# Decays as pinned steps of the SSD order, and a third buffer for split weights, in a hybrid Conformer, Mamba-2 and PEER step

## The chip, the cores and the metric

The kernel runs on one core of a Trainium2 chip. Its time is device time in microseconds, the median of several runs of the whole program: 1510.69 us over three runs, from 1509.24 to 1513.67. Profiled executions have a time and a span of their own, given below.

## What is computed

One step of a hybrid decoder layer on 336 token columns: 8 running sequences of 8 new tokens each (64 columns), 16 meta tokens and one prompt of 256 tokens. The layer normalises the input, projects it once, runs two branches, gates and adds them, and then runs a PEER expert mixer. Cut to what matters here, in the order of the reference:

```python
proj = rmsnorm(x, norm1_w) @ w_in + b_in          # 80 blocks of 128 columns, and dt
glu_in, z, xbc, dt_raw, gate_raw = split(proj)
u = ga * sigmoid(gb)                              # Conformer branch: GLU, 31-tap depthwise
c = silu(layernorm(causal_depthwise(concat(conf_buf, u), conf_dw_w, conf_dw_b)))
xbc_c = silu(causal_depthwise(concat(mconv_buf, xbc)))   # Mamba-2 branch: 4 taps, then SSD
acs = cumsum(dt * A)
decay = exp(where(causal, acs[:, None] - acs[None], -inf))
y_diag = einsum('btsgr,bsgrp->btgrp', cb[..., None] * decay, dt * x)
y_off  = einsum('btgn,bgrpn->btgrp', Cc, hc) * exp(acs)
h_new  = exp(last) * hc + einsum('bsgn,bsgrp->bgrpn', Bc, w_end * dt * x)
y_b = gated_group_rmsnorm(y + D * x, z, m_norm_w) @ w_m_out
x = x + (g_a * y_a + g_b * y_b) @ w_o
x = x + peer(rmsnorm(x, norm2_w))
```

There are 8 SSD groups of 4 heads; a head is 64 wide and the state 128.

## The kernel before

Activations lie with features on the partitions and the 336 token columns along the free axis. Every projection is one 128-wide block of weights (512 KB) against the normalised input. To keep fp32 accuracy both sides are split in a high and a low part (tiles `wh` and `wl`, `ah` and `al`): `weight` (L237) loads the block to `wraw` (4 buffers), ScalarE casts it to `wh`, and GpSimd, or for a share of the blocks VectorE, subtracts to make `wl`; both have 2 buffers. `proj` (L230) then issues 24 matmuls into one of three `pj` PSUM buffers: 16 that read `wh`, and 8 that read `wl`.

The middle of the kernel is a loop over the 8 SSD groups. In it three threads of work are woven by hand. A generator `ssd(g)` yields between its steps. The next group's conv branch (`conf(g+1)`: a value and a gated projection, then a 31-tap convolution on VectorE, L393, of which all but the first group's is given a low priority) and its four `xbc` blocks (projection, 4-tap convolution L408, Silu) and two `z` blocks are called between the steps. So one projection stands between two steps. The old group's last two steps (its second state update, its part of the group norm) run at the start of the next group. In the eighth group, where there is no next one, gate projections and the layer norm of the conv branch take that place (`norm_mean`, `norm_var`, `norm_scale`).

A scheduler places the instructions on the engines. Three rules bind it. Inside the loop `mm` and `tr` (L149, L154) keep PE's matmuls and transposes in the order in which the program calls them (`pin`). `act` (L194) chains those ScalarE activations that need a function table in program order. All else (VectorE, GpSimd, plain ScalarE copies) is placed by the scheduler.

The decays: `decays(g)` (L492) builds, for each of the 4 heads, a PSUM tile `pdec` by two matmuls (L498, L499; a broadcast of the cumulated dt, and the causal mask), which three Exps turn into `dec`; then two more tiles (L506) for the growth factors `e2`. `pdec` shares two PSUM buffers (tag `y`) with the outputs `py` and `po` of a group, so a third decay matmul waits until the first head's Exps have read theirs. These matmuls are called by `nc.tensor.matmul`, not by `mm`, so they are not pinned; `decays(g+1)` is called after the first xbc step of group g+1, a whole group ahead, and `dec` and `e2` have two buffers.

The steps of `ssd`: `turn(i)` transposes x and B of token tile i (`ptr`) and makes `xt` (x times dt, on ScalarE, L532) and `wx` (on GpSimd); `inner(i)` multiplies `dec` by C B^T (`pcb`, L545); `state(i)` makes the prompt's running states `hs` (`pst`, L557); `running` applies the cached states `st` to C (`pq`) and decays them on GpSimd (L569); `out(b)` makes the outputs (`py`, `po`, L585, L587); `update(q)` adds to the cached states (L599). All of these small PSUM tiles but `pdec`, `py` and `po` share two `misc` buffers. At the end `gnorm_stats` (L644) makes the group norm's factors from the sums `pgn` of all groups, and `gnorm` broadcasts them (`pgb`) and applies them.

## Time and profile before

| | us |
|---|---|
| median of 3 runs | 1510.69 |
| the profiled execution's own time | 1508.3 |
| its span | 1506.5 |
| the seven loop groups with a next group | 81 to 463 |
| the eighth group, with the first gates | 463 to 505 |
| gates, output projections (PE full from 556) | 505 to 700 |

The span is the time from the first to the last instruction; the execution's own time is 1.8 us longer. PE is TensorE's matmuls, PEld its weight loads, which run beside matmuls, DVE VectorE, ACT ScalarE, POOL GpSimd, SP the engine that issues most DMAs. A row of a timeline gives the start in us from the span's start, the length in us, the engine, the line, the operation, the tiles written and read with their shape, and, in brackets, how long the engine had stood idle before and what released it. A matmul's row lasts longer than the distance to the next, since matmuls are pipelined; the distance is what counts. In a table of waits each row is the waiting engine and line, what it waited for, and the total in us, the number of times and the longest. In a table by stage the granted clock is TensorE's, as a share of full speed.

### The profile page before, as it was taken

The numbers are of one execution on the slowest core, as the hardware profiler recorded it, in microseconds if no ns is written. First come the engines' busy times: TensorE is split into PE (matmuls) and PEld (weight loads), VectorE is DVE, ScalarE is ACT, GpSimd is POOL, SyncE is SP. The second block draws the span as 40 slices with busy tenths as digits, with TensorE's granted clock in tenths as the row PEclk, the third lists the DMA queues.
The fourth block names the chain that finished last, engine by engine and source line by source line (L and its number), as shares of the span: only waits on it lengthen the run. The fifth ranks groups of instructions, "written<-read, shape, count | busy, mean of one in ns | idle before, by whom it ended". The sixth has DMA issues, their size and how long they took to land.

```text
span 1506.5 us, 24647 instructions
## 1 busy us (share of the span) xinstructions
PE 1356.1 (90%) x9308; PEld 1272.0 (84%) x9308; DVE 1008.8 (67%) x2350; ACT 540.2 (36%) x1441; POOL 575.2 (38%) x467
## 2 busy tenths in 40 slices
PE   5878877977979799999999988999988999987997
PEld 3767766866867699998989987999988999987997
DVE  6765675675582751256999997677788868776423
ACT  4666566576564744343422222112111101111001
POOL 2236545645656366575322133213223112242100
PEclk9879889989989899999999999999999999999999
DMA  5414234234333234444499989999999999999983
GB/s 192 153 61 158 83 120 165 74 133 144 106 127 113 74 131 148 142 143 158 141 394 414 414 331 416 415 403 364 417 380 417 409 368 375 383 417 416 413 333 104
DMA packets 86807, 382.05 MB, mean 254 GB/s; under 512 B 10112, under 2 KB 15360, under 8 KB 66080
## 3 DMA queue, kind: packets, MB, share of 16 engines
q1 hardware_dynamic: 64144, 226.87, 41.2%
q0 software_dynamic: 20736, 151.00, 24.6%
q10 hardware_dynamic: 1808, 2.60, 0.5%
q8 instruction: 73, 1.20, 0.3%
q14 instruction: 46, 0.38, 0.1%
HBM read 367.41 MB, written 13.03 MB: 253 GB/s over the span
## 4 chain that ended last, share of the span: by engine, by line
PE 49%; DVE 12%; DMA 7%; ACT 1%; issue 1%; POOL 0%; DVEq 0%; POOLq 0%; ACTq 0%
PE va L1277 18%; PE pj L150 14%; PE pj L1186 10%; PE pg L1215 4%; DMA eraw<-in_vE_dram 3%; DMA eraw<-in_uT_dram 3%; DVE ygat L1120 2%; DVE wuv L1112 2%; DMA nd<-x1d 1%; DVE si L922 1%; DVE cand L965 1%; PE psc L1022 1%; DVE si L919 0%; DVE cand L959 0%; DVE cand L962 0%
## 5 line engine op out<-in xcount | busy, mean ns | idle before, releaser
L1000 POOL DMA_INDIRECT wuv<-in_peer_uv_dram,gid x144 | 180.1, 1251 | 513.0 <-DVE ygat L1120 221.8
L215 POOL TENSOR_TENSOR wl<-wraw,wh 128x1024 fp32r<-128x1024 f32 x115 | 275.3, 2394 | 262.4 <-PE pj L150 125.5
L1186 PE MATMUL pj<-nd,eraw 128*128 128x176 f32 x2048 | 321.5, 316 | 12.0 <-DMA eraw<-in_uT_dram 9.1
L1277 PE MATMUL va<-S,eraw 128*128 128x176 f32 x2048 | 315.2, 314 | 12.7 <-DMA eraw<-in_vE_dram 12.7
L1186 PEld LDWEIGHTS pj<-nd,eraw 128*128 128x128 f32 x2048 | 308.0, 191 | 16.2 <-ACT S L1188 7.6
L1277 PEld LDWEIGHTS va<-S,eraw 128*128 128x128 f32 x2048 | 306.1, 190 | 17.6 <-DMA eraw<-in_vE_dram 15.9
L150 PE MATMUL pj<-ah,wh 128*128 128x336 f32 (+1 forms) x768 | 260.0, 346 | 2.1 <-ACT xnf L195 2.1
L150 PE MATMUL pj<-al,wh 128*128 128x336 f32 (+1 forms) x768 | 250.6, 333 | 0.0
L214 ACT CAST wh<-wraw 128x1024 fp32r<-128x1024 f32 x128 | 134.5, 1050 | 200.5 <-PE pj L150 120.9
L1120 DVE SCALAR_TENSOR_TENSOR ygat<-wuv,scg,ygat 128x1024 f32<-128x1024 f32 x128 | 164.0, 1281 | 50.8 <-ACT scg L1115 50.6
L1112 DVE SCALAR_TENSOR_TENSOR wuv<-wuv,x2m 128x1024 f32<-128x1024 f32 x128 | 156.0, 1219 | 40.2 <-DMA wuv<-in_peer_uv_dram,gid 40.2
L1114 ACT ACTIVATE scg<-scg 128x1 f32<-128x1 f32 x144 | 29.1, 202 | 411.5 <-DVE wuv L1112 411.4
L150 PEld LDWEIGHTS pj<-ah,wh 128*128 128x128 f32 x768 | 156.8, 204 | 15.1 <-issue 5.9
L150 PEld LDWEIGHTS pj<-al,wh 128*128 128x128 f32 x768 | 156.6, 204 | 1.0 <-DVE al L215 0.5
L393 DVE SCALAR_TENSOR_TENSOR pcv<-ccat,vec,pcv 128x272 f32<-128x272 f32 x464 | 146.6, 392 | 9.8 <-ACT pcv L391 9.8
L150 PE MATMUL pj<-ah,wl 128*128 128x336 f32 (+1 forms) x768 | 138.4, 319 | 0.0
L150 PEld LDWEIGHTS pj<-ah,wl 128*128 128x128 f32 x768 | 122.7, 189 | 0.8 <-issue 0.7
L1188 ACT ACTIVATE S<-pj 128x176 f32<-128x176 f32 x128 | 37.5, 311 | 148.0 <-PE pj L1186 148.0
L1215 PE MATMUL pg<-oh 128*128 128x64 bf16 x1056 | 75.7, 241 | 0.0
L1215 PEld LDWEIGHTS <-oh 128*128 128x128 bf16 x1056 | 71.2, 117 | 2.3
L1222 DVE TENSOR_TENSOR S<-S,pg 128x192 f32<-128x192 f32 (+1 forms) x66 | 31.6, 507 | 56.7 <-PE pg L1215 56.6
L498 PE MATMUL pdec<-acs,id 96*128 96x336 bf16 x32 | 11.9, 375 | 58.6 <-ACT dec L195 58.5
(345 smaller groups left out, 1750.4 us busy)
## 6 DMA issues: line engine op xcount, KB each, us to landing
eraw<-in_uT_dram SPq DMA_DIRECT2D x128, 512.0 KB, 13.2
eraw<-in_vE_dram SPq DMA_DIRECT2D x128, 512.0 KB, 9.3
wraw<-in_w_in_dram SPq DMA_DIRECT2D x80, 512.0 KB, 3.6
st<-in_state_dram SPq DMA_DIRECT2D x8, 1024.0 KB, 5.2
out_ssm_s_dram<-st SPq DMA_DIRECT2D x8, 1024.0 KB, 6.5
wraw<-in_w_mo_dram SPq DMA_DIRECT2D x16, 512.0 KB, 3.4
wraw<-in_w_q_dram SPq DMA_DIRECT2D x16, 512.0 KB, 3.4
wraw<-in_w_co_dram SPq DMA_DIRECT2D x8, 512.0 KB, 3.5
```

Of the source, the lines that this page charges most:

```text
L150: i_ = nc.tensor.matmul(*a_, **kw)
L214: (nc.vector.tensor_copy if on_dve else nc.scalar.copy)(h, src)
L215: (nc.gpsimd if on_pool else nc.vector).tensor_tensor(l, src, h.bitcast(F32), op=OP.subtract)
L393: t = nc.vector.scalar_tensor_tensor(o, i_, wv, a_, op0=OP.mult, op1=OP.add)
L1000: i_ = nc.gpsimd.indirect_dma_start(out=u, out_offset=None, in_=ia["peer_uv"], in_offset=bass.IndirectOffsetOnAxis(ap=gid[:, c:c + 1], axi ...
L1112: nc.vector.scalar_tensor_tensor(u[:, :D], u[:, :D], 1.0, x2m if c < NPICK else x2e, op0=OP.mult, op1=OP.mult, accum_out=w)
L1120: nc.vector.scalar_tensor_tensor(a_, u[:, D:], scg[:, c:c + 1], a_, op0=OP.mult, op1=OP.add)
L1186: i_ = nc.tensor.matmul(p[:, :ND], raw[:, k, :], nd[:, k, :], start=(k == 0), stop=(k == KD - 1))
L1188: nc.scalar.activation(Sv(b), p[:, :ND], AF.Gelu)
L1215: i_ = nc.tensor.matmul(pg[:, q, :], B[:, q // 4, :, q % 4], A[:, c_, q // 4, :, q % 4], start=(c_ == 0), stop=(c_ == 2))
L1222: nc.vector.tensor_tensor(sv_, sv_, pg.rearrange("p t i -> p i t")[:, i0:i1], op=OP.mult)
L1277: i_ = nc.tensor.matmul(va[k // 2][:, k % 2], raw[:, k, :], Sv(b), start=False, stop=(b == 127), skip_group_check=True)
```

## The change

The changed kernel computes the same. Six things differ.

1. `decays(g)` is gone. Inside `ssd(g)` stand `decay(r)` for one head and `growth(b)` for two, with `mm`, so their matmuls are pinned. The first two heads are the generator's first step, before the conv-value projection of the next group; the other two come behind `turn(0)`, after it; the two growth tiles behind `turn(2)`, after the gated projection. `dec` and `e2` have one buffer.
2. The other steps are dealt out anew: `turn(1)` and `turn(2)` together, `running` with `inner(0)`, then one `inner` and one `state` at a time. The old group's last update and its norm sum fall one projection later than before.
3. In `turn`, x times dt is one VectorE product over 4 heads where it was four ScalarE activations. In `state`, four VectorE operations per tile become one GpSimd product and one VectorE add.
4. `weight` puts the split parts of each third block in a tile pair of their own (`wh3`, `wl3`) in the pool `sp`, where the second buffers of `dec` and `e2` were.
5. In the eighth group four gates stand between the first steps, `norm_var` is cut in two, and `norm_scale` and the seventh gate come before the last two updates, not after the loop.
6. `gnorm_stats` is called after the loop by itself, no longer inside `norm_scale`.

In the program as built the line numbers of the changed kernel differ by a few; pinned decay matmuls carry L150, the line of `mm`.

On PE, inside a group of the loop. Before, at the third head of the next group (`pcb` is the group's last inner product, `pj` the projection of the first xbc block ahead of it):

```order
L150 MATMUL pj<-ah,wl 128x336 x8
L150 MATMUL pcb<-bc 128x128 x2
L498 LDWEIGHTS id_256
L498 MATMUL pdec<-acs_247,id_256 128x336
L499 LDWEIGHTS identb
L499 MATMUL pdec<-mneg,identb 128x336
```

In the changed kernel, at the third head of the group itself (`pst` is the old group's second state update, `pj` the conv-value projection, `ptr` the transposes of the first token tile):

```order
L150 MATMUL pj<-ah,wl 128x336 x8
L150 MATMUL pst_1239<-wx_712,Bm 128x256
L150 MATMUL pst_1240<-wx_712,Bm 128x256
L150 MATMUL pst_1239<-wx_712,Bm 128x256
L150 MATMUL pst_1240<-wx_712,Bm 128x256
L155 MATMUL ptr<-cst,xg 80x128 x2
L155 MATMUL ptr<-cst,bc 80x128
L150 LDWEIGHTS id_256
L150 MATMUL pdec<-acs_247,id_256 128x336
L150 LDWEIGHTS identb
L150 MATMUL pdec<-mneg,identb 128x336
```

The third head has moved from behind the first xbc projection of the group before to behind the first projection of its own group.

On ScalarE, what stands ahead of the first head's Exps. Before (`xg` is the Silu of the first xbc block; `pj<-mcat` starts its convolution, which VectorE finishes):

```order
L406 ACTIVATE pj<-mcat,vec 128x360
L195 ACT_TABLE_LOAD
L195 ACTIVATE xg<-pj 128x272
L195 ACTIVATE xg<-pj 128x64
L195 ACT_TABLE_LOAD
L195 ACTIVATE dec<-pdec,acs_199 128x80
```

In the changed kernel (`sz` is the Silu of the second z block, `sq` a square for the old group's norm):

```order
L639 ACTIVATE sq<-xg 128x336
L195 ACTIVATE sz<-pj,vec 128x336
L195 ACT_TABLE_LOAD
L195 ACTIVATE dec<-pdec,acs_199 128x80
L195 ACTIVATE dec<-pdec,acs_224 128x128
L195 ACTIVATE dec<-pdec,acs_240 128x128
```

The Exps have moved from behind a Silu that needs VectorE to behind one that reads a projection.

On VectorE, at the turn from one group to the next. Before (`st` are the four adds of the state updates, `ccat` the start of the conv branch):

```order
L599 TENSOR_TENSOR st<-st,pst_1794 128x512
L599 TENSOR_TENSOR st<-st,pst_1795 128x512
L599 TENSOR_TENSOR st<-st,pst_1833 128x512
L599 TENSOR_TENSOR st<-st,pst_1834 128x512
L641 TENSOR_TENSOR pgn<-pgn 8x336
L477 SCALAR_TENSOR_TENSOR ccat<-pj,vec,xnf 128x272
```

In the changed kernel (`cbuf` are the last taps of the long convolution, `xt` the new products):

```order
L395 SCALAR_TENSOR_TENSOR cbuf<-ccat,vec,pcv 128x272
L395 SCALAR_TENSOR_TENSOR cbuf<-ccat,vec,pcv 128x64
L597 TENSOR_TENSOR st<-st,pst_1239 128x512
L597 TENSOR_TENSOR st<-st,pst_1240 128x512
L532 TENSOR_TENSOR xt_1252<-ptr,dtok_193 80x256
L644 COPY pgn<-pgn 8x336
L479 SCALAR_TENSOR_TENSOR ccat<-pj,vec,xnf 128x272
L480 SCALAR_TENSOR_TENSOR ccat<-pj,vec,xnf 128x8x8
L532 TENSOR_TENSOR xt_1389<-ptr,dtok_218 128x256
L532 TENSOR_TENSOR xt_1398<-ptr,dtok_234 128x256
```

The long convolution's taps, which ended in the middle of a group before, now reach to the second state update, and the xt products stand beside the conv branch's start.

The diff:

```diff
--- before.py
+++ after.py
@@ -237,15 +237,16 @@
         def weight(src, i):
             raw = wp.tile([128, KD, 128], F32, name="wraw", bufs=rb[0])
             nc.sync.dma_start(raw, src[i].rearrange("p (k m) -> p k m", m=128))
-            h = wp.tile([128, KD, 128], F32R, name="wh", bufs=2)
-            l = wp.tile([128, KD, 128], F32R, name="wl", bufs=2)
+            third = extra and nw[0] % 3 == 2
+            h = extra[0].tile([128, KD, 128], F32R, name="wh3") if third else wp.tile([128, KD, 128], F32R, name="wh", bufs=2)
+            l = extra[0].tile([128, KD, 128], F32R, name="wl3") if third else wp.tile([128, KD, 128], F32R, name="wl", bufs=2)
             nw[0] += 1
             f_ = lm[0]
             on_dve = int((nw[0] + 1) * f_) > int(nw[0] * f_)
             split(h, l, raw, on_pool=not on_dve, on_dve=lm[0] == 1)
             return h, l
 
-        lm, nw = [LM[3]], [NW0]
+        lm, nw, extra = [LM[3]], [NW0], []
 
         def rows(h, l):
             return lambda k: (h[:, k, :], l[:, k, :])
@@ -364,6 +365,7 @@
...
+        extra.append(sp)
...
@@ -489,34 +491,33 @@
...
-        def decays(g):
-            dec = sp.tile([128, 4, T], F32, name="dec", bufs=2)
-            e2 = sp.tile([128, 2, T], F32, name="e2", bufs=2)
-            for r in range(4):
-                h = 4 * g + r
-                pb = ps.tile([128, T], F32, name="pdec", tag="y", bufs=2)
-                nc.tensor.matmul(pb, id3[:, h:h + 1].to_broadcast([3 * H, 128]), acs3, start=True, stop=False)
-                nc.tensor.matmul(pb, identb, mneg, start=False, stop=True)
-                for i, (t0, L) in enumerate(TILES):
-                    act(dec[:, r, t0:t0 + L], pb[:, t0:t0 + L], AF.Exp, bias=acs[i][:, h:h + 1])
-            for b in range(2):
-                pb = ps.tile([128, T], F32, name="pdec", tag="y", bufs=2)
-                for r in range(2):
-                    h = 4 * g + 2 * b + r
-                    nc.tensor.matmul(pb[r * 64:(r + 1) * 64], id3[:, h:h + 1].to_broadcast([3 * H, 64]), acs3,
-                                     start=True, stop=True)
-                act(e2[:, b], pb, AF.Exp)
-            return dec, e2
-
         def r4(ap):
             return ap.rearrange("p (r c) -> p r c", r=4)
 
-        def ssd(g, xg, bc, sz, dec, e2):
+        def ssd(g, xg, bc, sz):
             BT, CT = bc[:, 0, :], bc[:, 1, :]
             st = sp.tile([128, NQ, 256], F32, name="st", bufs=2)
             nc.sync.dma_start(st, ia["state"][g])
             cz = cq[g % 2]
             xt, wx, hs = [], [], []
+            dec = sp.tile([128, 4, T], F32, name="dec")
+            e2 = sp.tile([128, 2, T], F32, name="e2")
+
+            def decay(r):
+                h = 4 * g + r
+                pb = ps.tile([128, T], F32, name="pdec", tag="y", bufs=2)
+                mm(pb, id3[:, h:h + 1].to_broadcast([3 * H, 128]), acs3, start=True, stop=False)
+                mm(pb, identb, mneg, start=False, stop=True)
+                for i, (t0, L) in enumerate(TILES):
+                    act(dec[:, r, t0:t0 + L], pb[:, t0:t0 + L], AF.Exp, bias=acs[i][:, h:h + 1])
+
+            def growth(b):
+                pb = ps.tile([128, T], F32, name="pdec", tag="y", bufs=2)
+                for r in range(2):
+                    h = 4 * g + 2 * b + r
+                    mm(pb[r * 64:(r + 1) * 64], id3[:, h:h + 1].to_broadcast([3 * H, 64]), acs3,
+                       start=True, stop=True)
+                act(e2[:, b], pb, AF.Exp)
...
@@ -528,9 +529,8 @@
...
-                for r in range(4):
-                    nc.scalar.activation(x_[:L, r * P:(r + 1) * P], p[:L, r * P:(r + 1) * P], AF.Copy,
-                                         scale=dtok[i][:L, 4 * g + r:4 * g + r + 1])
+                nc.vector.tensor_tensor(r4(x_[:L, :256]), r4(p[:L, :256]),
+                                        dtok[i][:L, 4 * g:4 * g + 4, None].to_broadcast([L, 4, P]), op=OP.mult)
...
@@ -552,10 +552,8 @@
                 if i == 0:
                     nc.vector.tensor_copy(h_, p)
                 else:
-                    for r in range(4):
-                        c_ = slice(r * P, (r + 1) * P)
-                        nc.vector.scalar_tensor_tensor(h_[:, c_], hs[-1][:, c_], el[:, 8 + i, 4 * g + r:4 * g + r + 1],
-                                                       p[:, c_], op0=OP.mult, op1=OP.add)
+                    nc.gpsimd.tensor_tensor(r4(h_), r4(hs[-1]), decay_b(8 + i), op=OP.mult)
+                    nc.vector.tensor_tensor(h_, h_, p, op=OP.add)
                 hs.append(h_)
 
             def running():
@@ -598,28 +596,35 @@
                     sv = st[:, 4 * s_ + q:4 * s_ + q + 2].rearrange("p q c -> p (q c)")
                     nc.vector.tensor_tensor(sv, sv, pair_[s_], op=OP.add)
 
+            decay(0)
+            decay(1)
+            yield
             turn(0)
+            decay(2)
+            decay(3)
+            yield
             turn(1)
+            turn(2)
+            growth(0)
+            growth(1)
             for s_ in range(2):
                 nc.scalar.copy(cz[:, 4 * s_:4 * s_ + 4, 8 * s_:8 * s_ + 8],
                                CT[:, 32 * s_:32 * s_ + 32].rearrange("p (q t) -> p q t", q=4))
             yield
-            turn(2)
+            running()
             inner(0)
             yield
             inner(1)
+            state(0)
+            yield
             inner(2)
-            yield
-            state(0)
-            running()
-            yield
             state(1)
-            state(2)
-            nc.sync.dma_start(oa["ssm_p"][g], hs[2])
             Bm = sp.tile([S0, 4, N], F32, name="Bm")
             for r in range(4):
                 nc.scalar.activation(Bm[:, r], xt[0][:S0, 256:], AF.Copy, scale=C("segs", S0)[:, r:r + 1])
             yield
+            state(2)
+            nc.sync.dma_start(oa["ssm_p"][g], hs[2])
             out(0)
             yield
             out(1)
@@ -698,15 +703,15 @@
                 nc.scalar.activation(sq, cb[:, k, :], AF.Square)
                 squares.append(sq)
 
-        def norm_var():
-            pv.append(pj())
-            for k in range(KD):
+        def norm_var(ks):
+            if not pv:
+                pv.append(pj())
+            for k in ks:
                 mm(pv[0], ones, squares[k], start=(k == 0), stop=(k == KD - 1))
 
         def norm_scale():
             rs = tp.tile([128, T], F32, name="rs", bufs=2)
             rstd_of(rs, pv[0], D, tp)
-            r24.append(gnorm_stats())
             for k in range(KD):
                 nc.vector.tensor_tensor(cb[:, k, :], cb[:, k, :], rs, op=OP.mult)
                 act(cb[:, k, :], cb[:, k, :], AF.Silu, scale=V("ln_g", k), bias=V("ln_b", k))
@@ -723,59 +728,47 @@
         (tiles, steps), (sz, zsteps) = xbc(0), zproj(0)
         for f in steps + zsteps:
             f()
-        de = decays(0)
         lm[0] = LM[0]
         pin[0] = True
         old = iter(())
         for g in range(G):
-            new = ssd(g, *tiles, sz, *de)
+            new = ssd(g, *tiles, sz)
             if g + 1 < G:
-                ca, cg = conf(g + 1)
-                ca()
+                tiles, steps = xbc(g + 1)
+                tasks = conf(g + 1) + steps
+            else:
+                lm[0] = LM[1]
+                tasks = [lambda: gate(len(gates))] * 4
+            run(old, 1)
+            run(new, 1)
+            for f in tasks:
+                f()
                 run(old, 1)
                 run(new, 1)
-                cg()
-                run(old, 1)
-                run(new, 1)
-                tiles, steps = xbc(g + 1)
-                steps[0]()
-                run(new, 1)
-                de = decays(g + 1)
-                steps[1]()
-                run(new, 1)
-                steps[2]()
-                run(new, 1)
-                steps[3]()
-                run(new, 1)
+            if g + 1 < G:
                 sz, zsteps = zproj(g + 1)
                 zsteps[0]()
                 run(new, 1)
                 zsteps[1]()
-                run(new, 1)
                 old = new
             else:
-                lm[0] = LM[1]
-                gate(0)
-                run(old, 2)
-                run(new, 2)
-                gate(1)
-                run(new, 2)
-                gate(2)
-                run(new, 1)
-                gate(3)
-                run(new, 1)
                 norm_mean()
                 gate(4)
                 run(new, 1)
+                norm_var(range(4))
+                run(new, 1)
                 gate(5)
                 run(new, 1)
-                norm_var()
-                run(new, 2)
+                norm_var(range(4, KD))
+                norm_scale()
+                gate(6)
+                run(new, 3)
         nc.scalar.dma_start(oa["mconv"], mnew)
         ls.close()
+        extra.clear()
 
         m2 = mix.enter_context(tc.tile_pool(name="m2", bufs=1))
-        norm_scale()
+        r24.append(gnorm_stats())
         while len(gates) < NB:
             gate(len(gates))
         for g in range(G):
```

## The prediction

> **What bounds the kernel now.** I read the page first, then the table of waits, then busy times by stage, then the rows of one group. The profiled execution took 1508.3 us, its span 1506.5 us; the sum is made against 1508.3 and the median of the three runs, 1510.69, lies 2.4 us above it.
>
> ```profile
> PE 1356.1 (90%) x9308; PEld 1272.0 (84%) x9308; DVE 1008.8 (67%) x2350; ACT 540.2 (36%) x1441; POOL 575.2 (38%) x467
> ```
>
> PE is the engine to watch. Its waits, over the whole span, are led by one entry (line waited at, releaser: total us, times, longest); the third row is from the same table for all engines between 80 and 480 us:
>
> ```profile
> PE pdec L498 <- ACT dec L195: 58.5, 8, 8.5
> PE pgb L150 <- DVE acs L225: 8.2, 1, 8.2
> ...
> ACT xg L195 <- DVE pj L408: 19.5, 7, 3.2
> ```
>
> Eight times PE stands before a decay matmul for ScalarE's Exp. Busy time by stage (length, then PE, PEld, DVE, ACT, POOL, granted clock) for three of the seven loop groups and a stretch well behind them:
>
> ```profile
> 81.00:135.70 54.70, 45.66 (x300) 40.06 (x299) 34.28 (x95) 33.62 (x90) 30.51 (x30) 0.88 0.26 85
> 190.30:245.00 54.70, 46.09 (x296) 39.46 (x297) 34.28 (x96) 33.95 (x90) 30.91 (x31) 0.91 0.37 123
> 408.70:463.00 54.30, 45.36 (x292) 39.03 (x291) 33.89 (x97) 35.19 (x89) 29.58 (x27) 0.91 0.38 130
> ...
> 556.00:700.00 144.00, 143.67 (x942) 142.86 (x941) 56.63 (x70) 62.05 (x88) 92.05 (x47) 1.00 0.48 157
> ```
>
> A loop group takes (463.0 − 81.0) / 7 = 54.6 us, and no engine is busy for more than 46 of them. Behind 556 us PE is full at clock 1.00, so what the loop saves moves everything later forward by as much. Why PE stands there is read on ScalarE (start, us, engine, line, operation, then idle before and its releaser):
>
> ```profile
> 96.51 0.51 ACT L195 ACTIVATE xg<-pj 128x272 f32<-128x272 f32 x2 [3.20 <-DVE pj L408]
> 97.02 1.28 ACT L195 ACT_TABLE_LOAD   x1
> 98.32 1.57 ACT L195 ACTIVATE dec<-pdec,acs 128x80 f32<-128x80 f32 x6
> ```
>
> The Exps of the next group's first two heads stand behind the Silu of that group's first xbc tile, which waits for VectorE's short convolution, itself between taps of the long one. Two PSUM buffers hold two heads, so PE stops at the third. What a stop costs, in one group, beside one projection at full clock (the first three rows):
>
> ```profile
> 53.95 0.32 PE L150 MATMUL pj<-ah,wh 128*128 128x336 f32 x1
> 56.43 1.40 PE L150 MATMUL pj<-ah,wl 128*128 128x336 f32 x8
> 57.67 0.32 PE L150 MATMUL pj<-ah,wh 128*128 128x336 f32 x1
> ...
> 188.37 1.13 PE L150 MATMUL pst<-wx,Bm 32*128 32x256 f32 x8
> 189.43 0.32 PE L498 MATMUL pdec<-acs,id 96*128 96x336 bf16 x1
> 189.58 0.31 PE L499 MATMUL pdec<-mneg,identb 128*128 128x336 bf16 x1
> ...
> 208.83 0.44 PE L498 MATMUL pdec<-acs,id 96*128 96x336 bf16 x1 [7.88 <-ACT dec L195]
> 211.63 0.65 PE L150 MATMUL pj<-ah,wh 128*128 128x336 f32 x1
> 216.00 1.40 PE L150 MATMUL pj<-ah,wl 128*128 128x336 f32 x8
> ```
>
> A projection is 24 matmuls in 57.67 − 53.95 = 3.72 us; its first 16 take 2.48. After the 7.88 us stop the same 16 take 216.00 − 211.63 = 4.37, a loss of 1.9: PE runs slow for some 6 us. The eight decay matmuls take 2.80 where 8 x 0.15 (the spacing at 189.43) and a hop of 0.1 would be 1.3, a loss of 1.5. So a stop costs 7.88 + 1.9 + 1.5 = 11.3 us, and a group without one 54.6 − 11.3 = 43.3 us.
>
> The Trainium skill (TensorE: Matmul & The Clock Gate, on HAM oscillation) says that PE's clock halves after an idle window of some 3.4 us and comes back after a busy one. The trace agrees on the halving, not on the length of the slow stretch, 6 us here.
>
> **The change part by part.** *Decays as steps.* The same matmuls are issued, pinned, as pairs of heads with one projection between: heads 0 and 1 before the conv-value projection, 2 and 3 after it, the growth rows after the gated one. Now the Exps of heads 0 and 1 follow the Silu of the second z tile, with no VectorE work ahead of them. The same run of ScalarE work exists before the first group:
>
> ```profile
> 69.94 0.56 ACT L195 ACTIVATE sz<-pj,vec 128x336 f32<-128x336 f32 x1
> 70.51 1.28 ACT L195 ACT_TABLE_LOAD   x1
> 71.81 3.23 ACT L195 ACTIVATE dec<-pdec,acs 128x80 f32<-128x80 f32 x12
> ```
>
> Silu, load and half of the twelve Exps are 0.56 + 1.28 + 1.6 = 3.4 us, 5.0 with a weight cast (1.05) and a square (0.48) ahead. PE's cover until the third head: the update before (188.37 to 189.43, 1.06), heads 0 and 1 (0.6), a projection (3.72), the second update (1.06) and one set of transposes (0.6), 7.0 us. That leaves 2.0 us, so the stop goes. Heads 2 and 3 have the gated projection as cover for 1.6 us of Exps; the growth Exps are not needed before the outputs, four projections later. Table loads stay four a group: Exp, Sigmoid, Exp, Silu, where it was Sigmoid, Silu, Exp, Silu. One buffer for dec and e2 instead of two costs nothing: the next group's first Exp comes after the last output's matmuls and one projection (3.72).
>
> The Trainium skill (ScalarE: Activation LUTs, What ACT_TABLE_LOAD costs) gives 1.28 us for a load and 1.38 more for a drain. The trace has the load at 1.28 and the next activation 0.02 later (70.51, 71.81). By the skill's figure the margin of 2.0 would be an estimated 0.6, and the sum the same.
>
> *Who takes over work.* Groups of rows for 190.3 to 245.0 us (count, busy, mean ns, idle before):
>
> ```profile
> L393 DVE SCALAR_TENSOR_TENSOR pcv<-ccat,vec,pcv 128x272 f32<-128x272 f32 (+1 forms) x58 | 18.3, 393 | 1.1 <-ACT pcv L391 1.1
> L599 DVE TENSOR_TENSOR st<-st,pst 128x512 f32<-128x512 f32 x5 | 3.3, 683 | 8.0 <-PE pst L150 8.0
> L557 DVE SCALAR_TENSOR_TENSOR hs<-hs,el,pst 128x64 f32<-128x64 f32 x8 | 1.6, 278 | 0.4 <-PE pst L150 0.4
> L641 DVE TENSOR_TENSOR pgn<-pgn 8x336 f32<-8x336 f32 x1 | 0.5, 493 | 5.0 <-PE pgn L150 5.0
> L553 DVE COPY hs<-pst 128x256 f32<-128x256 f32 x1 | 0.4, 425 | 1.2 <-PE pst L150 1.2
> L569 POOL TENSOR_TENSOR st<-st,el 128x256 f32<-128x256 f32 x8 | 4.6, 619 | 0.0
> L532 ACT ACTIVATE xt<-ptr,dtok 128x64 f32<-128x64 f32 (+1 forms) x12 | 2.8, 322 | 0.0
> ```
>
> No row shows VectorE's new 256-wide product out of PSUM; the copy L553 has that width and source. Bounds are 0.28 (one L557) and 0.68 (512 wide, L599); I take 0.42. VectorE: + 3 x 0.42 for xt, − 1.6 for the eight state steps, + 2 x 0.42 for the two adds: 34.3 becomes 34.8 us. ScalarE loses 2.8: 34.0 becomes 31.2. GpSimd gains 2 x 0.62: 30.9 becomes 32.1. Against 43.3 that is 80%, 72% and 74%.
>
> *The third set of split weights* removes no PE wait, since none of PE's waits names wh or wl; it keeps any from coming. On GpSimd a state product now stands ahead of a weight split and waits for VectorE's add; with a third set that split is a whole projection early (3.72), more than the 0.62 of the product and an add of 0.42.
>
> *VectorE's order* is the part that is not free. Between the second state update and the conv branch's ccat it holds only an xt product and the pgn add, 1.0 to 2.2 us of work with the update's own adds, while PE needs two transposes, two heads, a projection and ScalarE's Sigmoid, some 6 us: 4 us idle each group. The other 32.6 us must fit into 43.3 − 6.0 = 37.3, a margin of 4.7 for all other hand-overs. VectorE is idle for 20.4 us of a group today; half of that would make 34.8 + 10.2 = 45.0. I take 44.7, 1.4 above PE's floor: the bounds are 43.3 and the 50.1 of three quarters, and it lies nearer the floor because the taps now stand between the hand-overs to the group's end. Loop: 7 x (54.6 − 44.7) = 69.3 us.
>
> *Start and end.*
>
> ```profile
> 72.70 0.44 PE L498 MATMUL pdec<-acs,id 96*128 96x336 bf16 x1 [3.12 <-ACT dec L195]
> 75.50 0.65 PE L150 MATMUL pj<-ah,wh 128*128 128x336 f32 x1
> 79.69 1.40 PE L150 MATMUL pj<-ah,wl 128*128 128x336 f32 x8
> ...
> 463.56 0.73 PE L150 MATMUL pgn<-sq,cstm 128*8 128x336 f32 x2 [0.86 <-DVE st L599]
> 465.91 0.44 PE L155 MATMUL ptr<-cst,xg 128*128 128x128 f32 x2 [0.49 <-ACT xt L532]
> 468.03 0.40 PE L150 MATMUL pcb<-bc 128*80 128x80 f32 x2 [1.57 <-ACT xt L532]
> 468.59 0.48 PE L150 MATMUL pj<-al,wh 128*128 128x336 f32 x1
> ```
>
> The eighth stop, before the first group, costs 3.12, then 2.80 − 1.3 and (79.69 − 75.50) − 2.48: 6.3 us; I take 5, since what starts the loop stays. In the last group the transposes wait 2.9 us for ScalarE and VectorE, and the slow projection behind adds about 1.4; spread steps remove most, 3. Against that the wait before pgb, 8.2: a gate projection stood behind the last group's end as its cover (3.72) and now stands before it, and the statistics' Ln and Exp come behind the norm's eight Silus and two table loads (2 x 1.28 at most). I take 2 us lost there, between 4 lost and 1 won. End: 1 gained.
>
> Sum: 69.3 + 5 + 1 = 75.3; 1508.3 − 75.3 = 1433.0, and 2.4 for the median: **1435.4 us**.
>
> **The rivals.** *VectorE binds.* For it: 80% busy, in order, with PE's transposes waiting for its state adds. Against: taps fill its gaps. With three quarters of today's idle time its group is 50.1 us; gains 7 x 4.5 + 6 = 37.5, so 1508.3 − 37.5 + 2.4 = 1473.2. It decides from 4.7 us of hand-overs on. By the skill's clock rule, single waits under 3.4 us leave the clock alone; the rows from 463.56 to 468.59 show three of 0.5 to 1.6 us and then half speed (0.28 us from 468.59 to the next), so I keep slow stretches in this rival.
>
> *Two stops for one, slower.* Place: the third head's matmul and the first growth one, which both wait for a PSUM buffer that an Exp must free. If ScalarE comes to the Silu more than 2.0 us late, PE stops, and if it stops at both, each group has two stops at today's price: 7 x 11.3 = 79 us more, 1508.3 + 79 + 2.4 = 1590. For it: ScalarE is in order and its weight casts wait for PE. Against: a third set frees a cast's buffer a projection earlier.
>
> *No change.* The order moves but the stop returns elsewhere at its old size, or the later stage takes the time back: 1510.7. Against it: PE at 143.67 of 144.00 us.
>
> **How the numbers follow.** Forecast 0.78, VectorE binds 0.14, no change 0.03, two stops 0.05. Best case: 7 x 11.3 + 6.3 + 4 = 89.4, so 1421; with the start's unknown order 1419. The range goes from there into the first rival, to 1474. Beyond 0.3% (4.5 us, about what a measurement of this kernel can tell): faster 0.92, same 0.03, slower 0.05.
>
> **What would show it.** Right: PE's wait at pdec under 6 us in all; group starts 44 to 46 us apart; the granted clock above 0.96 through the loop; four table loads a group; VectorE busy some 35 us a group; pgb still waiting 8 to 12 us. Wrong: groups over 48 us, PE's waits led by a transpose or state matmul behind VectorE, or clock rows still near 0.91.

## The result and the profile after

The changed kernel takes 1439.25 us (median of four runs, 1437.99 to 1442.71); the kernel before, on the same chip, 1510.24. The ratio is 0.953, with a 95% interval from 0.9506 to 0.9553. The forecast was 1435.4. Two executions among those of the versions below, one of 4575.13 us (third set late) and one of 3342.22 (no third set), were far slower than all others of their kernels, and the ratios leave them out.

The profiled execution of the changed kernel took 1442.71 us, the slowest of its four, with a span of 1440.9 and a mean granted clock of 0.973 (0.957 before). By stage, cut where PE issues the first transposes of the first and of the eighth group and the first and last output projection (the first is the one that reads `yh`, the last the one that reads `mh`):

| stage | before, us | after, us | difference |
|---|---|---|---|
| start to the first group | 80.9 | 83.4 | +2.5 |
| seven loop groups | 383.3 | 303.15 | −80.1 |
| eighth group to the first output projection | 81.5 | 88.9 | +7.4 |
| output projections | 128.4 | 128.4 | 0.0 |
| the rest, with the same code | 832.4 | 837.0 | +4.6 |

Without the last row the stages sum to −70.2, and the medians differ by 71.0. The 4.6 us of the rest are put down to these two executions: the one of the changed kernel was 3.5 us above its median, the one of the kernel before 1.9 below.

In the table of PE's waits of the changed kernel (line waited at, releaser: total, times, longest) the entry at `pdec` that led it is gone; the first of these rows was 8.2 before, the other three are new:

```profile
PE pgb L150 <- DVE acs L225: 12.0, 1, 12.0
PE ptr L155 <- DVE st L597: 5.7, 7, 1.0
PE pst L150 <- DVE st L597: 5.0, 1, 5.0
PE pj L150 <- ACT wh L214: 4.7, 1, 4.7
```

Busy time by stage after (length, then PE, PEld, DVE, ACT, POOL, granted clock): the loop, one group of it, the eighth group, and the stretch of the statistics and the last gates.

```profile
83.40:386.50 303.10, 296.83 (x2064) 261.79 (x2062) 236.05 (x646) 222.26 (x544) 217.97 (x217) 1.00 0.46 150
169.10:212.70 43.60, 42.52 (x295) 37.36 (x295) 34.50 (x94) 31.69 (x78) 30.55 (x32) 1.00 0.47 154
386.50:434.00 47.50, 41.99 (x264) 34.52 (x265) 22.69 (x40) 26.16 (x50) 24.83 (x24) 0.95 0.29 92
434.00:475.40 41.40, 27.39 (x154) 25.44 (x154) 26.71 (x47) 25.61 (x48) 17.30 (x12) 0.77 0.23 77
```

The loop, at clock 0.90 before, runs at 1.00 now, and PE is busy for 42.5 of a group's 43.6 us. ScalarE's rows of one group show why no head waits; the first two heads' matmuls were issued from 162.79 on, the last of them at 163.23:

```profile
160.59 1.05 ACT L214 CAST wh<-wraw 128x1024 fp32r<-128x1024 f32 x1 [2.42 <-PE pj L150]
161.93 0.52 ACT L195 ACTIVATE sz<-pj,vec 128x336 f32<-128x336 f32 x1
162.46 1.28 ACT L195 ACT_TABLE_LOAD   x1
163.75 1.57 ACT L195 ACTIVATE dec<-pdec,acs 128x80 f32<-128x80 f32 x6
```

The Silu is over before the first of these matmuls; the table load ends 0.2 us after the last one (163.23 + 0.31). Both heads' buffers are free at 165.32, and PE comes to the third head 4.1 us later, 0.8 of them a wait in the transposes. The third head needs the first head's buffer alone, which is free some 0.8 us earlier (half of 1.57, an estimate):

```profile
161.72 1.13 PE L150 MATMUL pst<-wx,Bm 32*128 32x256 f32 x8
...
167.17 1.13 PE L150 MATMUL pst<-wx,Bm 32*128 32x256 f32 x8
169.08 0.42 PE L155 MATMUL ptr<-cst,xg 128*80 128x128 f32 x2 [0.78 <-DVE st L597]
169.33 0.27 PE L155 MATMUL ptr<-cst,bc 128*80 128x128 f32 x1
169.44 0.31 PE L150 MATMUL pdec<-acs,id 96*128 96x336 bf16 x1
```

### The profile page after: what moved, and what is told of

Same layout as the page of the kernel before. It is cut to its first block, busy times and chain, and to the rows that moved or that the text cites. A ratio compares the mean times of both kernels' runs of the same rounds, so it can differ in the third digit from the quotient of the medians.

```text
span 1440.9 us, 24529 instructions
## 1 busy us (share of the span) xinstructions
PE 1333.8 (93%) x9308; PEld 1260.0 (87%) x9308; DVE 1004.4 (70%) x2326; ACT 525.9 (36%) x1347; POOL 587.3 (41%) x483
## 4 chain that ended last, share of the span: by engine, by line
PE 74%; DVE 14%; DMA 8%; ACT 2%; issue 1%; POOL 0%; DVEq 0%; SPq 0%; ACTq 0%
PE pj L150 31%; PE va L1270 19%; PE pj L1179 11%; PE pg L1208 4%; DMA eraw<-in_vE_dram 3%; DMA eraw<-in_uT_dram 3%; PE pst L150 2%; DVE ygat L1113 2%; DVE wuv L1105 2%; PE pdec L150 1%; PE po L150 1%; DMA nd<-x1d 1%; PE py L150 1%; PE ptr L155 1%; DVE si L915 1%
## 5 line engine op out<-in xcount | busy, mean ns | idle before, releaser
L993 POOL DMA_INDIRECT wuv<-in_peer_uv_dram,gid x144 | 184.2, 1279 | 513.1 <-DVE ygat L1113 217.5
L1179 PEld LDWEIGHTS pj<-nd,eraw 128*128 128x128 f32 x2048 | 309.7, 192 | 16.7 <-ACT S L1181 11.8
L150 PE MATMUL pj<-ah,wh 128*128 128x336 f32 (+1 forms) x768 | 249.7, 334 | 6.7 <-ACT wh L214 4.7
L150 PE MATMUL pj<-al,wh 128*128 128x336 f32 (+1 forms) x768 | 241.0, 322 | 0.0
L395 DVE SCALAR_TENSOR_TENSOR pcv<-ccat,vec,pcv 128x272 f32<-128x272 f32 x464 | 151.6, 388 | 17.7 <-ACT pcv L393 17.7
L150 PEld LDWEIGHTS pj<-ah,wh 128*128 128x128 f32 x768 | 148.0, 193 | 16.7 <-ACT wh L214 4.8
L150 PEld LDWEIGHTS pj<-al,wh 128*128 128x128 f32 x768 | 148.3, 193 | 1.1 <-DVE al L215 0.5
L150 PE MATMUL pj<-ah,wl 128*128 128x336 f32 (+1 forms) x768 | 138.0, 319 | 0.0
L150 PEld LDWEIGHTS pj<-ah,wl 128*128 128x128 f32 x768 | 122.4, 189 | 0.8 <-issue 0.7
L1181 ACT ACTIVATE S<-pj 128x176 f32<-128x176 f32 x128 | 37.7, 312 | 156.4 <-PE pj L1179 156.3
L1215 DVE TENSOR_TENSOR S<-S,pg 128x192 f32<-128x192 f32 (+1 forms) x66 | 31.7, 507 | 53.0 <-PE pg L1208 52.7
L410 DVE SCALAR_TENSOR_TENSOR pj<-mcat,vec,pj 128x360 f32<-128x360 f32 x96 | 55.9, 586 | 1.2 <-ACT pj L408 1.2
```

What stands on the lines that cost most here:

```text
L150: i_ = nc.tensor.matmul(*a_, **kw)
L395: t = nc.vector.scalar_tensor_tensor(o, i_, wv, a_, op0=OP.mult, op1=OP.add)
L410: nc.vector.scalar_tensor_tensor(o, cat[:, w:w + n], wv, o, op0=OP.mult, op1=OP.add)
L993: i_ = nc.gpsimd.indirect_dma_start(out=u, out_offset=None, in_=ia["peer_uv"], in_offset=bass.IndirectOffsetOnAxis(ap=gid[:, c:c + 1], axi ...
L1179: i_ = nc.tensor.matmul(p[:, :ND], raw[:, k, :], nd[:, k, :], start=(k == 0), stop=(k == KD - 1))
L1181: nc.scalar.activation(Sv(b), p[:, :ND], AF.Gelu)
```

## The experiments

The theory: the gain is the loop's, and the decays' new place on PE and ScalarE makes it; the third set of split weights, the engine moves and the new end are worth little or cost time. The rivals: the parts need each other; the Exps' place on ScalarE is enough by itself; VectorE is about to bind. Ratios are to the kernel before in the same session.

**What carries the loop's gain.** First the engine moves taken back, in two edits:

```diff
-                nc.vector.tensor_tensor(r4(x_[:L, :256]), r4(p[:L, :256]),
-                                        dtok[i][:L, 4 * g:4 * g + 4, None].to_broadcast([L, 4, P]), op=OP.mult)
+                for r in range(4):
+                    nc.scalar.activation(x_[:L, r * P:(r + 1) * P], p[:L, r * P:(r + 1) * P], AF.Copy,
+                                         scale=dtok[i][:L, 4 * g + r:4 * g + r + 1])
...
-                    nc.gpsimd.tensor_tensor(r4(h_), r4(hs[-1]), decay_b(8 + i), op=OP.mult)
-                    nc.vector.tensor_tensor(h_, h_, p, op=OP.add)
+                    for r in range(4):
+                        c_ = slice(r * P, (r + 1) * P)
+                        nc.vector.scalar_tensor_tensor(h_[:, c_], hs[-1][:, c_], el[:, 8 + i, 4 * g + r:4 * g + r + 1],
+                                                       p[:, c_], op0=OP.mult, op1=OP.add)
```

> The changed kernel with x times dt on ScalarE again (12 activations a group) and the state steps on VectorE again (8 operations). Theory: these are not on PE's path; 43.4 to 44 us a group, 1438 to 1443. Rival: ScalarE's 2.8 us more a group delay the Exps and xt, so that PE waits again for pdec or ptr, 2 us or more a group: 1453 or more.

Measured: 1440.39 us, ratio 0.9537 (0.9522 to 0.9552). The loop takes 306.4 us, 3.3 more, and the wait of the transposes for VectorE grows from 5.7 to 7.4 us over the loop. Behind the longest of these waits, 1.62 us, the granted clock was 0.85 from 213.41 to 225.00, an estimated 1.7 us more:

```profile
PE ptr L155 <- DVE st L600: 7.4, 7, 1.6
```

Then the third set left out:

```diff
-        extra.append(sp)
```

> The changed kernel without the third pair of tiles at all. Theory (the decays as steps carry the gain): the loop stays at 43.4 to 43.8 us a group and the start is as in third_late, about 1433. Rival (the third set keeps weight splits ahead of PE, now that the group is a fifth shorter and GpSimd has state products ahead of splits): PE waits for wh or wl by 2 to 4 us a group, 1433 + 7 x 3 = 1454.

Measured: 1432.83 us, 0.9481 (0.9462 to 0.9499). The loop keeps its 303.3 us, the start is 8.3 us earlier. In the eighth group a wait appears that the kernels with a third set in the loop do not have (how the set removes it was not followed); from the group's start to the first output projection it takes 92.0 us instead of 88.9:

```profile
405.28 0.70 PE L150 MATMUL pst<-wx,xt 128*128 128x256 f32 x2 [2.10 <-DVE dec L544]
```

Then everything but the decays as steps and the new dealing of the steps taken back: both edits above, and the old end as well:

```diff
+            r24.append(gnorm_stats())
...
-                norm_scale()
-                gate(6)
...
-        r24.append(gnorm_stats())
+        norm_scale()
```

> The changed kernel with everything taken back but the decays as steps and the new dealing of the steps: no third set of split weights, x times dt on ScalarE and the state steps on VectorE as before, norm_scale, the group norm's statistics and the seventh gate after the loop as before. Theory (the decays' place between projections carries the loop's gain; the third set costs 6 us at the start and gains 4 in the eighth group, the engine moves are worth 0.5 us a group, the new end costs some 5 us): no_third's 1432.8, plus 3.3 for the loop's engine moves, minus 4 to 7 for the end: 1429 to 1434. The wait at pdec stays under 6 us in all, groups are 43.8 to 44.3 us apart. Rival (the parts need each other: with ScalarE's products back and no third set the third head stops PE again in some groups): stops of 1 to 3 us in several groups, 1440 to 1460.

Measured: 1429.51 us, 0.947 (0.9454 to 0.9485). So the decays and the steps around them carry the whole gain; all the rest together costs some 9 us (0.953 − 0.947 of 1511). The new dealing of the steps was not run without the decays, so how the two share the gain stays open. The row of one group:

```profile
161.11:204.87 43.76, 42.54 (x295) 37.40 (x295) 32.18 (x93) 33.43 (x89) 30.79 (x31) 1.00 0.46 154
```

**Is the Exps' place on ScalarE enough?** The kernel before, with one line moved, so that all decays stand ahead of the first xbc projection:

```diff
+                de = decays(g + 1)
                 steps[0]()
                 run(new, 1)
-                de = decays(g + 1)
```

> The kernel before with one line moved: decays of the next group called ahead of the first xbc step, not after it, so that in ScalarE's chain the Exps stand ahead of the Silu that waits for VectorE. Nothing is pinned and no step is dealt anew. Theory (the place in ScalarE's chain makes the stop): the stop of 7.9 us and the slow stretch go in most groups, 44 to 47 us a group, 1440 to 1460. Rival (it is the pinning and the new dealing of the steps that matter): stops of over 4 us stay, 1490 or more.

Measured: 1483.45 us, 0.9821 (0.9806 to 0.9836), between the two: groups of 51.1 us. The stop is smaller, and there are two of them, at the third head and at the growth tiles:

```profile
192.32 0.30 PE L498 MATMUL pdec<-acs,id 96*128 96x336 bf16 x1 [2.34 <-ACT dec L195]
193.06 0.30 PE L498 MATMUL pdec<-acs,id 96*128 96x336 bf16 x1 [0.29 <-ACT dec L195]
195.69 0.49 PE L506 MATMUL pdec<-acs,id 96*64 96x336 bf16 x2 [2.19 <-ACT dec L195]
196.43 0.49 PE L506 MATMUL pdec<-acs,id 96*64 96x336 bf16 x2 [0.24 <-ACT dec L195]
196.85 0.65 PE L150 MATMUL pj<-ah,wh 128*128 128x336 f32 x1
201.37 0.94 PE L150 MATMUL pj<-ah,wl 128*128 128x336 f32 x5
```

The waits sum to 5.1 us, and the first 16 matmuls behind take 4.5 instead of 2.48: together 7.1 of the 7.7 us above 43.4. So the place ahead of that Silu brought 27 of the 71 us. Is the rest the projection between the pairs of heads? The kernel before, still a group ahead, but with its decays called by `mm`, and `decays` a generator whose three parts are heads 0 and 1, heads 2 and 3, and the growth tiles:

```diff
+                dk = decays(g + 1)
+                de = next(dk)
+                run(dk, 1)
                 steps[0]()
                 run(new, 1)
-                de = decays(g + 1)
+                run(dk, 1)
...
                 steps[2]()
                 run(new, 1)
+                run(dk, 1)
```

> The kernel before, with the decays still made a whole group ahead, but pinned and spread: heads 0 and 1 ahead of the first xbc projection, heads 2 and 3 behind it, the growth tiles two projections later. Nothing else is changed, dec and e2 keep two buffers; there are seven table loads a group instead of four. It asks what the rest of the loop's gain hangs on, since Exps moved earlier alone gave 27 of 71 us. Theory (a projection between pairs of heads is what removes the stop; whether the decays are made in their own group or one ahead does not matter): no wait at pdec over 1 us, groups of 43.5 to 45 us, 1434 to 1447. Rival (the decays must be in the group's own first steps, where ScalarE has no VectorE work ahead of the Exps; here the Exps of heads 2 and 3 still stand behind a Silu that VectorE releases): PE still waits at pdec, for the growth tiles, 2 to 5 us a group, 1455 to 1475.

Measured: 1483.64 us, 0.981 (0.9794 to 0.9827). Both missed, and the miss says more than either. The wait at `pdec` is indeed gone (0.3 us in the loop). But PE stops at the next user of the same two PSUM buffers, the output `py`, which must wait for the growth Exps `e`; these stand behind a Silu that VectorE releases (PE, then ScalarE):

```profile
218.84 1.39 PE L150 MATMUL py<-dec,xt 80*64 80x80 f32 x12 [4.44 <-ACT e L195]
```

```profile
216.53 0.51 ACT L195 ACTIVATE bc<-pj 128x272 f32<-128x272 f32 x2 [0.50 <-DVE pj L408]
217.04 1.28 ACT L195 ACT_TABLE_LOAD   x1
218.34 0.79 ACT L195 ACTIVATE e<-pdec 128x336 f32<-128x336 f32 x2
```

A group takes 51.2 us: 4.4 of the stop, 0.6 more at `pst`, some 2 of slow clock behind (granted 0.61 from 218.84 to 225.00), and 0.8 that stay unassigned. One of the seven table loads, 1.28 us, stands in the stop. While the decays are made a group ahead, then, neither half is enough: not the place ahead of the Silu, and not a projection between the pairs. In the group's own first steps, where the heads' Exps do not stand behind VectorE's work, the two are worth very different amounts, as the next run shows.

**How near the edge is it?** All four heads at once, with no projection between them:

```diff
             decay(0)
             decay(1)
-            yield
-            turn(0)
             decay(2)
             decay(3)
             yield
+            turn(0)
+            yield
```

> The changed kernel with all four heads' decay matmuls in the generator's first step, so no projection stands between the second head and the third. It is a probe of the margin of 2.0 us and of the price of a stop. With the projection (3.72 us) and the second update and transposes (1.66) gone from the cover, the third head waits: 7.0 of cover less 5.4 is 1.6 against ScalarE's 3.4 to 5.0, so a stop of 1.8 to 3.4 us, and the fourth head one of 0.8 more. Theory (a stop costs its own length and, where it or several close together slow the clock, 3.4 us more as in the old loop): groups of 47 to 50 us, 1465 to 1485. Rival (a stop under 3.4 us costs its own length only): groups of 45.5 to 47, 1454 to 1464. If the margin was much larger than 2.0 us, the stop is under 1 us and the time under 1447.

Measured: 1456.63 us, 0.9653 (0.9637 to 0.967); groups of 45.7 us in the mean. The cover taken away is 5.4 us and the wait 1.1 to 1.4, with 0.28 at the fourth head: so there were 4.0 to 4.3 us to spare, as read from the trace above. Without the projection between the pairs a group is still 9.0 us shorter than before (54.75 − 45.7), so that projection, with the update and the transposes beside it, is worth 2.4 of the 11.4 us. The rest is the new place, with the growth tiles two steps later and the other steps dealt out anew. The groups come in two lengths, 45.2 to 45.8 and 46.6 to 46.9, after waits of the same size. The third head's matmul in two such groups, and the stretch from there into the projection:

```profile
216.11 0.30 PE L150 MATMUL pdec<-acs,id 96*128 96x336 bf16 x1 [1.10 <-ACT dec L195]
261.52 0.30 PE L150 MATMUL pdec<-acs,id 96*128 96x336 bf16 x1 [1.10 <-ACT dec L195]
```

```profile
216.10:219.50 3.40, 3.11 (x20) 2.80 (x20) 1.94 (x7) 2.44 (x10) 1.47 (x3) 1.00 0.45 154
...
261.50:265.50 4.00, 3.69 (x14) 3.31 (x14) 1.95 (x7) 2.56 (x10) 1.47 (x3) 0.57 0.40 131
```

In the one the clock stays at 1.00, in the other it is 0.57 for 4 us. The time lies in the rival's range, but its reason (a short stop costs only itself) holds in some groups and not in others.

Next VectorE's margin, with the cached states' decay moved to it:

```diff
-                    nc.gpsimd.tensor_tensor(r4(st[:, q]), r4(st[:, q]), decay_b(q), op=OP.mult)
+                    nc.vector.tensor_tensor(r4(st[:, q]), r4(st[:, q]), decay_b(q), op=OP.mult)
```

> The changed kernel with the cached states' eight decay products of each group on VectorE, where they are GpSimd's: a probe of VectorE's margin. They add 8 x 0.42 to 8 x 0.5 = 3.4 to 4.0 us, so VectorE is busy 38 of a group's 43.4 us. Theory (the prediction's margin: VectorE has 8.9 us of idle time in a group, of which only some 4 to 5 must be idle): it still fits, or just not; groups of 43.4 to 44.2, 1439 to 1445. Rival (the rival of the prediction, hand-overs that hold some 10 us of VectorE's time, binds here): each us added lengthens the group, 45 to 47.5 us, 1450 to 1468.

Measured: 1476.04 us, 0.9767 (0.974 to 0.9793): groups of 48.5 us, longer than the rival said. The products take 30.0 us in seven groups, 4.3 in each, and VectorE is busy for 37.7 of the 47.4 us of the group shown; groups take 46.6 to 51.7 (the group of rows from 80 to 430 us, and one group by stage):

```profile
L567 DVE TENSOR_TENSOR st<-st,el 128x256 f32<-128x256 f32 x56 | 30.0, 593 | 0.0
```

```profile
180.45:227.81 47.36, 42.84 (x295) 37.29 (x295) 37.67 (x100) 31.09 (x78) 26.98 (x24) 1.00 0.42 143
```

They stand in two blocks between the running states and the first inner product, for which PE's state matmul waits (VectorE's rows, then PE's):

```profile
193.58 2.27 DVE L567 TENSOR_TENSOR st<-st,el 128x256 f32<-128x256 f32 x4
195.78 0.69 DVE L395 SCALAR_TENSOR_TENSOR pcv<-ccat,vec,pcv 128x272 f32<-128x272 f32 x2
196.38 1.42 DVE L567 TENSOR_TENSOR st<-st,el 128x256 f32<-128x256 f32 x4
197.72 0.47 DVE L545 TENSOR_TENSOR dec<-dec,pcb 80x320 f32<-80x320 f32 x1
```

```profile
198.34 0.66 PE L150 MATMUL pst<-wx,xt 16*128 16x256 f32 x2 [1.68 <-DVE dec L545]
204.68 0.42 PE L150 MATMUL pj<-ah,wh 128*128 128x336 f32 x1 [1.11 <-ACT xg L195]
```

4.3 us of work cost 5.2 a group; over the seven groups PE waits 16.7 us at this `pst` and 7.7 at this `pj`. Here idle time on VectorE was no margin for a block that lands ahead of a hand-over; whether the same work in small pieces would fit was not tried.

**The start.** After the change PE waits there for a weight cast (PE, then ScalarE):

```profile
36.01 0.22 PE L326 MATMUL pdt<-cst,dt 32*80 32x32 f32 x1 [3.01 <-DVE dt L315]
52.05 0.65 PE L150 MATMUL pj<-ah,wh 128*128 128x336 f32 x1 [4.66 <-ACT wh L214]
```

```profile
50.96 1.04 ACT L214 CAST wh<-wraw 128x1024 fp32r<-128x1024 f32 x1
```

The third weight is the first to go to `wh3`, whose memory belonged to the dt work until then: in the chain of work that ended last, VectorE's last `acs` row of that work (50.23, 0.34 us long) stands right ahead of this cast. The edit lets the third set begin with the loop:

```diff
-        extra.append(sp)
...
         lm[0] = LM[0]
+        extra.append(sp)
         pin[0] = True
```

> The changed kernel, with the third pair of tiles given to weight only just before the loop, so that no weight of the prologue uses it. Theory: the third set does nothing in the loop but costs at the start, since its memory is that of the dt scope, and the first xbc block's cast waits until the dt work is over (PE's wait of 4.7 us for wh, then slow clock). Then the loop keeps 43.4 us a group and starts 6 to 8 us earlier: about 1432. Rival: the start is late because the scheduler packed the dt matmuls together; then the time stays at 1439, within 2 us.

Measured: 1428.18 us, 0.9447 (0.9427 to 0.9467); the first group starts at 74.0 instead of 83.4, the loop takes 303.24 as in the changed kernel. The third projection now ends where the dt matmuls begin (its last matmul stands at 36.30 us) and fills the wait of 3.01 us at `pdt`.

**The end.** Rows of VectorE and of ScalarE in the changed kernel, around the last updates and the statistics:

```profile
424.75 5.59 DVE L716 TENSOR_TENSOR cbuf<-cbuf,rs 128x336 f32<-128x336 f32 x8
430.26 1.27 DVE L597 TENSOR_TENSOR st<-st,pst 128x512 f32<-128x512 f32 x2
```

```profile
436.18 1.28 ACT L195 ACT_TABLE_LOAD   x1 [4.30 <-DVE rsv L204]
437.47 0.48 ACT L195 ACTIVATE rst<-rsv 8x336 f32<-8x336 f32 x1
437.97 1.28 ACT L195 ACT_TABLE_LOAD   x1
439.26 0.48 ACT L195 ACTIVATE rst<-rst 8x336 f32<-8x336 f32 x1
```

The norm's eight products stand ahead of the state add for which PE waits 5.0 us, and two table loads stand on the chain to `pgb`. One edit puts the norm, with `gnorm_stats` inside, and the seventh gate back behind the loop; the other loads one table for Ln and Exp ahead of the statistics:

```diff
+            r24.append(gnorm_stats())
...
                 norm_var(range(4, KD))
-                norm_scale()
-                gate(6)
                 run(new, 3)
...
-        r24.append(gnorm_stats())
+        norm_scale()
```

> The changed kernel with the norm's eight products and Silus, the group norm's statistics and the seventh gate after the loop as they were before, and the last two updates right behind the variance. Theory (the end lost some 8 us because norm_scale's eight products stand on VectorE ahead of the last state add and the statistics have lost their cover): the wait at pst of 5.0 us goes, the one at pgb falls from 12.0 to about 8.2, the distance from the eighth group's start to the first output projection falls from 88.9 to 80 to 83 us, 1430 to 1434. Rival (the end's loss is in the eighth group's steps and its spread of gates, not in the norm): 1437 to 1441.

```diff
-            rstd_of(r8, pgn, 256, tp, load=False)
+            rstd_of(r8, pgn, 256, tp)
```

> The changed kernel with one explicit table load (the one that holds both Ln and Exp) ahead of the group norm's statistics, where after the change there is a load for Ln, one for Exp behind it and one for the next Silu. Theory (the loads for Ln and for Exp stand on the chain to pgb and the first waits for the sum before it is issued): with one load issued ahead, both come off the chain, the wait at pgb falls from 12.0 to about 9.4, and the time by 2.6 to 3.5 us: 1435.5 to 1437. Rival (VectorE's and GpSimd's work behind the statistics ends last anyway): pgb's wait stays near 12, 1439.

Measured: 1435.22 us (0.9513, 0.9497 to 0.9529) and 1433.80 us (0.9509, 0.9491 to 0.9527). Their intervals overlap the changed kernel's, so the traces decide. With one load the wait falls from 11.96 to 9.40 us, by two loads of 1.28 as expected, and the eighth group to the first output projection takes 85.7 us instead of 88.9:

```profile
443.41 0.72 PE L150 MATMUL pgb<-acs,id 96*128 96x336 bf16 x2 [9.40 <-DVE acs L225]
```

The Trainium skill (ScalarE: Activation LUTs, Table sets: the hidden batching unit) counts a single load for Ln and then Exp, by a set that holds both. The changed kernel's trace has two there, and only a kernel that asks for that set has one.

With the norm behind the loop the wait at `pst` falls to 0.77 and that at `pgb` to 6.45, but the eighth group to the first output projection takes 85.8 us, where 80 to 83 were expected. The eight products now stand ahead of the sum that the statistics read:

```profile
426.42 3.43 DVE L717 TENSOR_TENSOR cbuf<-cbuf,rs 128x336 f32<-128x336 f32 x8
429.77 0.48 DVE L646 TENSOR_TENSOR pgn<-pgn 8x336 f32<-8x336 f32 x1
```

**A version that beats both.** First the third and fourth head ahead of the transposes, since the heads have time to spare and the transposes wait:

```diff
-            turn(0)
             decay(2)
             decay(3)
+            turn(0)
             yield
```

> The changed kernel with the third and fourth head's decay matmuls ahead of the first transposes of the group instead of behind them. Theory (the third head has several us to spare, as the stop of only 1.1 to 1.4 us with all heads together shows, and the transposes wait 0.78 us a group for VectorE's state add): the 0.6 us of decay matmuls cover that wait, it falls to 0.1 to 0.2 us, groups from 43.4 to 42.8 us, 4 us less in all: 1434 to 1436, ratio about 0.950. Rival (the margin of the third head is the 2.0 us of the prediction, and the transposes were part of its cover): the third head begins to wait in some groups, no gain, 1439 or more.

Measured: 1436.25 us, 0.9506 (0.9489 to 0.9522), again within the interval of the changed kernel; but the trace has groups of 42.7 us (299.1 for seven), and one wait of 0.34 us at `ptr` is left of seven. Then this, the late third set, and an end with the statistics first:

```diff
-        extra.append(sp)
...
+        extra.append(sp)
         pin[0] = True
...
                 norm_var(range(4, KD))
-                norm_scale()
-                gate(6)
                 run(new, 3)
...
-            rstd_of(r8, pgn, 256, tp, load=False)
+            rstd_of(r8, pgn, 256, tp)
...
-            rstd_of(rs, pv[0], D, tp)
+            rstd_of(rs, pv[0], D, tp, load=False)
...
         while len(gates) < NB:
             gate(len(gates))
+        norm_scale()
```

> Three edits of the changed kernel together: the third set of split weights is used from the loop on only; the third and fourth head's decay matmuls stand ahead of the first transposes; behind the loop come first the group norm's statistics with one table load, then the seventh gate, then the norm's products and Silus. Theory (the start's 9.4 us, the loop's 7 x 0.6 and the end's 5 to 8 us add up): the ratio of 0.9447 of the first edit alone becomes 0.937 to 0.940, 1415 to 1420. The wait at pgb is under 5 us. Rival (the norm's products then come too late for the projections behind the gates, or the statistics' chain is as long as before): 1421 to 1425.

Measured: 1415.49 us, 0.938 (0.9362 to 0.9397), some 23 us under the changed kernel (0.953 − 0.938 of 1511). The first group starts at 74.7, seven groups take 299.3, the eighth to the first output projection 78.0 where it was 88.9. No wait for the statistics is left at `pgb`; what is left there is the hand-over of `xg`:

```profile
PE pgb L150 <- DVE xg L661: 5.1, 2, 3.6
```

## Why the prediction was right, step by step

The time was right to 3.9 us, and the mechanism held: the stop at `pdec` is gone and the loop runs at clock 1.00. That the number came so near is in part luck. The loop gained 10.8 us more than forecast, and the start and the end together 15.9 less.

- **The floor of a group, 54.6 − 11.3 = 43.3 us.** Measured 43.3 (303.15 / 7), but with PE's wait of 0.78 us in the transposes in it. The version with the third and fourth head ahead of the transposes has one such wait left in the whole loop, at clock 1.00, and takes 42.7. So without waits a group is some 0.6 us shorter than the floor, and the whole price of a stop is 54.75 − 42.7 = 12.0, not 11.3; where the other 0.7 goes stays open.
- **44.7 a group, 69.3 us in all.** Mis-sized: the loop gained 80.1, and the groups are 43.3 us apart, below the 44 to 46 given as a sign. Of the 1.4 us for VectorE's hand-overs some 0.6 came (43.3 − 42.7, PE's wait in the transposes), and the floor was as much too high.
- **A margin of 2.0 us at the third head.** Measured 4.0 to 4.3 by the run with all heads together, and 4.1 in the trace. The cover was right: from the first update at 161.72 to the third head at 169.44, less the wait, 6.9 against 7.0. ScalarE's path was too long. The weight cast is over at 161.64, before the cover begins, and the third head needs three Exps, of the first head, not the six in the sum.
- **Prices and shares.** The new product x times dt takes 0.42 us and the new add 0.41, as taken from L553. VectorE, ScalarE and GpSimd are busy 34.5, 31.7 and 30.6 us of a group, against 34.8, 31.2 and 32.1; four table loads. The engine moves as a whole are worth 0.5 us a group in the profiles, and in the time nothing clear of the spread (1440.39 without them against 1439.25).
- **The third set "removes no PE wait … it keeps any from coming".** In the loop none came without it either (303.3 us); in the eighth group it saves 3 to 4 us. What failed is the next step, "I take 5, since what starts the loop stays": the set adds a user to memory that the dt work still holds. The first stop did go (with the late third set the loop starts 7.0 us earlier than before), but 9.4 us were lost to the cast: 2.5 lost in place of 5 gained.
- **The end, 1 us gained.** Lost 7.4. Of the 2.9 us that were put down to the transposes only 0.49 stood there; 0.86 was the norm sum's wait and 1.57 that of `pcb`. They did mostly go: 0.78 at the transposes and 0.28 at the norm sum are left. `pgb` rose by 3.8, just inside the bound of 4. What the sum missed is the wait of 5.0 at `pst`: `norm_scale` was moved ahead of the last updates, and its eight products, 5.59 us, came to stand ahead of a state add on VectorE. The step named the queue on ScalarE that the statistics were moved past, not the one on VectorE. The clock is 1.00 until that wait begins, and 0.50 from its end at 430.99 to the end of the one at `pgb`, 447.17.
- **The rivals.** "VectorE binds" did not happen. The run with 4.3 us more on VectorE shows it near, and nearer than a sum of busy and idle time would have it: most of the loss stands at two hand-overs right behind the added blocks. "Two stops for one" is what the version with only the Exps' place changed looks like, in a milder form: two smaller stops, at the third head and at the growth tiles.

## What to carry to other kernels

Look at every user of a shared buffer: when one is freed of the slow chain and another is not, the stop can move to that one, as it moved here from `pdec` to `py`. When a step is moved, list what it is put ahead of on each in-order engine, and who waits there. A new tile in reused memory can inherit the waits of the old owner, as `wh3` did: start it when that work is long over.

## What was not expected of the hardware

TensorE's clock dropped after stops of 1.10 and 0.28 us in one group (granted 0.57 over 4 us) and stayed at 1.00 over 3.4 us after stops of the same size in another group of the same execution; after the two short pairs in the run with the Exps first it was slow as well, with no wait over 2.4 us. The Trainium skill (TensorE: Matmul & The Clock Gate, What's actually happening) ties the drop to an idle window of some 3.4 us, and says that the window runs freely. No single wait in those groups is that long, so the trace does not bear out the length; that the same stop is charged in one group and not in the next fits a free-running window, but no run isolates that.

The same VectorE product took 0.43 us in the eight behind the loop (3.43) and 0.70 in the eight of the changed kernel (5.59). What stretched it was not tried.
